# Combining attention heads in six parts, one a slot, with one order of groups and retention outputs a slot later

## The chip, the cores and the metric

The kernel runs on one core of a Trainium2 chip. The metric is the time of one execution in microseconds (us) on the device. The program before took 2319.36 us, the median of three runs (2316.97 to 2319.66).

## The reference

One decoder block on 1024 tokens of width 1024, in fp32. Cut to what matters here:

```python
xn = rmsnorm(x, norm1_g)
qa, ka, va, qr, kr, vr, gr, gate_a, gate_b = split(xn @ w_in)
# mixer A: 12 heads of width 128, three groups of four: (window, dilation) = (128,1), (512,4), (2048,16)
for g in range(3):
    o[g], lse[g] = dilated_group(rmsnorm(qa)[g], rmsnorm(ka)[g], va[g], slopes[g], window[g], dilation[g])
alpha = softmax(stack(lse), axis=0)                    # over the three groups of a head slot
o_a = sum(alpha * stack(o), axis=0)                    # 4 slots of 128
# mixer B: 4 heads, chunks of 128 tokens
s = einsum(q, k) * decay                               # within the chunk: a mask of powers of the decay
out = s @ v + (q @ state) * xi                         # output of a chunk
state = state * g_chunk + (k * zeta).T @ v             # update
o_r = head_groupnorm(out, g, b) * silu(gr)
y = sigmoid(gate_a) * (o_a @ w_proj_a) + sigmoid(gate_b) * (o_r @ w_proj_b)
x = x + y @ w_out
x = x + relu(rmsnorm(x, norm2_g) @ w_up) ** 2 @ w_down
```

## The kernel before

Every large product is split: each fp32 operand is a sum of a high and a low part (`xh`, `xl`; `wh`, `wl`), and three matmuls (high by high, high by low, low by high) replace one. `split` makes the parts: ScalarE copies the high part (L287), VectorE subtracts it (L288). Weights stream from DRAM through three raw buffers and six split buffers (`W`), with 4 units for an attention head.

The stages follow one another: normalisation, attention, the gates, retention, projection a (of attention), projection b (of retention), the output projection, and the MLP.

TensorE's order is the program's. A `Pipe` gives it a form: each `pipe.step` is a slot, one accumulation group (24 matmuls in attention, 12 in projection a), and `pipe.at(lag, fn)` asks for small work that depends on an earlier group, such as transposes, scores and values, to be issued between the terms of the slot `lag` slots after the next. The other engines' instructions are ordered by a list scheduler that has its own estimates, so the place of a line in the program sets their order only loosely. SyncE issues the DMAs in that order, and each of these queues is worked off in order: an instruction that waits holds up what stands behind it.

Attention has 12 heads, in four slots of three groups (`heads`). A head has 8 blocks of 128 tokens. Its queries and keys are normalised (`qk`), turned (`turn_qk`, into `qT`, `kT`), and attended in three steps (scores with `s`, turn with `pr` and `pT`, values into `acc`) at lag 2 for group 0. For groups 1 and 2 the lag is 9, because V goes through DRAM (`v_d`) to get its dilated order (`Vd`). `store` writes `acc` to `acc_d` after the last block. When the three heads of a slot are stored, `load_heads` reads half of the tokens of all three back into `at` (four DMAs into one buffer), and `combine` weighs them by their denominators (`w`; its Exp is on ScalarE), mixes them (`oa`, on VectorE), and asks for their turn (`oaT`) and a store to `oa_d`. This is done in two halves in the last head of the next slot; the last slot's are done in the first head of retention.

Retention works through 4 heads of 8 chunks. For a chunk, `sm` is the masked score (`maskT`, L771), split into `smh` and `sml`; `qh`, `ql`, `kzh`, `kzl`, `vh`, `vl` are the other operands. `output` (9 matmuls and the start of the normalisation of `on`) and `update` (6 matmuls) run one slot after the chunk's values, `turn_o` one slot later still; `on` is then turned, gated and stored to `on_d`.

Projection a has 16 half-steps; each multiplies its product in `ms` by a gate tile `s0` (loaded from `sg_d` into four buffers; the profile calls the tile `s`) and stores it to `pa_d`. Beside it, `load_o` loads the rows of `on_d` (`oraw`, two buffers) and splits them for projection b.

Of the kernel before, what the change touches and what calls it, by code (L numbers as in the profile page):

```python
# [10 lines left out]
F = mybir.dt.float32  # L11
# [226 lines left out]
def hybrid_block(ctx: ExitStack, tc: tile.TileContext, a: dict, out: bass.AP):  # L238
# [62 lines left out]


    W = Weights(nc, rawp, wp, split)
    heads = [(slot, g) for slot in range(SLOTS) for g in ((0, 1, 2) if slot < SLOTS - 1 else (1, 2, 0))]
    for slot, g in heads:
        for u in range(4):
            W.add(a["w_att"][g * SLOTS + slot, u])
# [63 lines left out]
    def as_rows(slot):  # L371

        return [x.rearrange("p (s a) b -> p s (a b)", s=2) for x in slot]
# [28 lines left out]

    def combine(s, i, p2b, at):

        w = p2b.tile([P, 6, 4], F, name="w")
        nm = [at[:, :, g, DH] for g in range(3)]
        dn = [at[:, :, g, DH + 1] for g in range(3)]
        nc.vector.tensor_tensor(w[:, 5], nm[0], nm[1], op=OP.min)
# [11 lines left out]
        oa = p2b.tile([P, 4, DH], F, name="oa")  # L420
        for t in range(4):
            nc.vector.tensor_scalar(oa[:, t], at[:, t, 0, :DH], w[:, 0, t:t + 1], None, op0=OP.mult)
            for g in (1, 2):
                nc.vector.scalar_tensor_tensor(oa[:, t], at[:, t, g, :DH], w[:, g, t:t + 1], oa[:, t],
                                               op0=OP.mult, op1=OP.add)

        def turn():
            pt = tr.tile([P, 4, P], F, name="tr")
            for t in range(4):
                nc.tensor.transpose(pt[:, t, :], oa[:, t, :], ident)  # L430
            ot = p2b.tile([P, 512], F, name="oaT")
            nc.scalar.activation(ot, pt.rearrange("p t q -> p (t q)"), AF.Copy)
            nc.sync.dma_start(oa_d[s, :, 512 * i:512 * i + 512], ot)

        return turn


    attn = ExitStack()
# [3 lines left out]
    with ExitStack() as ph:  # L442
# [69 lines left out]
        for head, (slot, g) in enumerate(heads):  # L512
# [57 lines left out]
            for b in range(NT):  # L570
                if b == 1:
                    nc.vector.tensor_scalar(bias, dist[:, 0 if g < 2 else 1, :], -slope * (DIL[g] if g < 2 else 8),
                                            None, op0=OP.mult)
                if head == 0 and b + 2 < NT:
                    norm1(b + 2)
                if head == 1 and b == 4:
                    first.close()
                    cmb = pool(ph, "cmb", 2)
                if head in (4, 7, 10) and b == 6:
                    at = load_heads(head // 3 - 1, 0, cmb)  # L580
                if head in (5, 8, 11) and b in (0, 3):
# [12 lines left out]
                ss = p3.tile([P, 4], F, name="ssa")  # L594
                junk = p3.tile([P, P], F, name="junk")
                for j in range(2):
                    nc.scalar.activation(junk, pm[:, j * DH:(j + 1) * DH], AF.Square, accum_out=ss[:, j:j + 1])
                rsqrt(ss[:, 2:4], ss[:, 0:2], 1.0 / DH)
                qk = p3.tile([P, 2, DH], F, name="qk", bufs=3)
                nc.scalar.activation(V[:, b, :], pm[:, 2 * DH:3 * DH], AF.Copy)  # L600
                nc.vector.tensor_tensor(qk, pm[:, :2 * DH].rearrange("p (a d) -> p a d", a=2),
                                        ss[:, 2:4, None].to_broadcast([P, 2, DH]), op=OP.mult)

                def turn_qk(g=g, b=b, h=h, qk=qk, qT=qT, kT=kT):
                    pt = tr.tile([P, 4, P], F, name="tr")
# [12 lines left out]
                pipe.at(1, turn_qk)  # L618
            if g > 0:
# [4 lines left out]
                                          v_d[h, 512 * nb:512 * nb + 512, :].rearrange("(p r) e -> p r e", r=4))  # L624
                else:
                    nc.sync.dma_start(Vd, v_d[h].rearrange("(p r) e -> p r e", r=8))


    def gate_out(f, d, cs, src):
# [88 lines left out]
    with ExitStack() as ph:  # L718
# [1 line left out]
        p2 = pool(ret, "p22", 2, "right")  # L720
        p2b = pool(ph, "p22b", 2, "right")

        maskT = cp.tile([P, RH, P], F, name="maskT")
        nc.sync.dma_start(maskT, a["c_mask"])
        rc = const.tile([P, 3, RH], F, name="rc")
        nc.sync.dma_start(rc, a["c_ret"])

        gng = cp.tile([P, 2, NF], F, name="gng")
        nc.sync.dma_start(gng, a["ret_gn"])
        ready = {}  # L730

        def load_chunk(n):
# [22 lines left out]
        for h in range(RH):  # L755
# [4 lines left out]
            for c in range(NT):  # L760
# [5 lines left out]
                def decay(c=c, h=h, it=it, qT=qT, kT=kT):  # L766
# [2 lines left out]
                        nc.tensor.matmul(sp[:, :P], kT[:, f], qT[:, f], start=(f == 0), stop=(f == 1))  # L769
                    sm = p2b.tile([P, P], F, name="sm")  # L770
                    nc.vector.tensor_tensor(sm, sp[:, :P], maskT[:, h, :], op=OP.mult)  # L771
                    it["s"] = p2.tile([P, P], R, name="smh"), p2.tile([P, P], R, name="sml")
                    split(*it["s"], sm)
                    if c > 0:
                        it["q"] = p2.tile([P, 2, P], R, name="qh"), p2.tile([P, 2, P], R, name="ql")
                        split(*it["q"], qT)
                    if c < NT - 1:
                        pt = tr.tile([P, 4, P], F, name="tr")
                        for f in range(2):
                            nc.tensor.transpose(pt[:, f, :], kT[:, f], ident)  # L780
                        kzh = p2b.tile([P, 2, P], R, name="kzh")
                        kzl = p2b.tile([P, 2, P], R, name="kzl")
# [57 lines left out]
                it["v"] = p2.tile([P, DV], R, name="vh"), p2.tile([P, DV], R, name="vl")  # L840
                split(*it["v"], pm)
                pipe.at(0, output, update)
                pipe.at(1, turn_o)
                if h == 0 and c in (0, 2):
                    at = load_heads(SLOTS - 1, c // 2, p2b)
                if h == 0 and c in (1, 4):
                    pipe.at(3, combine(SLOTS - 1, c // 4, p2b, at))
                if h == RH - 1 and c >= 4:
                    load_oa(c - 4)


    before = XS[0, 0], XS[1, 0]
    oS = [x for i in range(2) for x in as_rows(XS[i, 1])]
    with ExitStack() as ph:
# [353 lines left out]
```

## Time and profile before

| | |
|---|---|
| median of the runs | 2319.36 us |
| the profiled execution | 2327.33 us, its span 2325.6 us |
| busy share of the span | TensorE 98%, VectorE 50%, ScalarE 40%, GpSimd 4% |
| mean granted clock of TensorE | 0.995 |
| moved by DMA | 303.19 MB, 130 GB/s |

In the lines below, a group or timeline line names line, engine, operation and tiles (output, arrow, inputs). In square brackets stands how long the engine was idle before it, and what ended that. `SPq` is SyncE issuing DMAs, `PEld` TensorE's weight loads. A line of DMA issues ends with KB each and the median us from issue to landing. A granted clock of 1.00 is full speed.

### The profile page before, as it was taken

To read this page: it belongs to the slowest core of one execution; us is meant where nothing else is said; L and a number is where in the kernel's file an instruction comes from. 1 tells how busy PE (TensorE), PEld (TensorE's weight loads), DVE (VectorE), ACT (ScalarE), POOL (GpSimd) and SP (SyncE) were. 2 spreads that over 40 slices of the span, in tenths; PEclk is the share of its full clock that TensorE was granted. 3 is DMA by queue.
4 is the path that set the end of the run, shared out by engine and by line. 5 is a ranking of instruction groups with operands and counts; after the bars stand their busy time and mean duration, and the time that the engine had idled before them with its cause. 6 is when DMAs were issued, how large, how long until landed. Compare 5 with 4: busy or idle time off the path is not lost. (4 is left out here: it accounts for less than half of the span.)

```text
span 2325.6 us, 29822 instructions
## 1 busy us (share of the span) xinstructions
PE 2281.0 (98%) x11060; PEld 1952.9 (84%) x11060; DVE 1165.8 (50%) x2356; ACT 926.2 (40%) x2078; POOL 104.0 (4%) x148
## 2 busy tenths in 40 slices
PE   8999999999999999989999999999999999999999
PEld 7999998998888888868888878888788888888887
DVE  6344445454644445557676752363855555233532
ACT  6444444445343333335455533122566666211010
POOL 1111111110000000000000000000000000000000
PEclk9999999999999999999999999999999999999999
DMA  4212322332233333363433385554254457733601
GB/s 140 82 55 74 105 63 78 96 105 91 68 112 112 117 113 109 100 187 104 123 113 100 104 273 180 164 171 163 83 173 166 167 169 271 288 127 133 234 28 73
DMA packets 186275, 303.19 MB, mean 130 GB/s; under 512 B 13457, under 2 KB 99601, under 8 KB 182034
## 3 DMA queue, kind: packets, MB, share of 16 engines
q1 hardware_dynamic: 186130, 301.29, 39.9%
q8 instruction: 87, 1.43, 0.3%
q14 instruction: 58, 0.48, 0.1%
HBM read 204.68 MB, written 96.57 MB: 130 GB/s over the span
## 5 line engine op out<-in xcount | busy, mean ns | idle before, releaser
L193 PE MATMUL mm<-wh,xh 128*128 128x384 f32 (+1 forms) x1536 | 605.1, 394 | 5.1 <-ACT wh L287 5.1
L193 PE MATMUL mm<-wh,xl 128*128 128x384 f32 (+1 forms) x1536 | 561.7, 366 | 2.4 <-DVE xl L288 2.1
L288 DVE TENSOR_TENSOR wl<-raw,wh 128x1024 fp32r<-128x1024 f32 (+2 forms) x282 | 306.6, 1092 | 423.1 <-ACT wh L287 420.1
L193 PE MATMUL mm<-wl,xh 128*128 128x384 f32 (+1 forms) x1344 | 486.6, 362 | 2.6 <-DVE wl L288 2.6
L287 ACT ACTIVATE wh<-raw 128x1024 fp32r<-128x1024 f32 (+2 forms) x282 | 267.2, 953 | 535.7 <-PE mm L193 272.1
L193 PEld LDWEIGHTS mm<-wh,xh 128*128 128x128 f32 x1536 | 291.5, 190 | 36.6 <-ACT wh L287 5.7
L193 PEld LDWEIGHTS mm<-wh,xl 128*128 128x128 f32 x1536 | 290.4, 189 | 35.5 <-DVE xl L288 3.4
L193 PE MATMUL mm<-xl,wh 128*128 128x512 f32 x848 | 309.7, 390 | 1.7 <-DVE xl L288 1.7
L193 PE MATMUL mm<-xh,wh 128*128 128x512 f32 x848 | 310.1, 390 | 0.0
L193 PE MATMUL mm<-xh,wl 128*128 128x512 f32 x720 | 280.7, 390 | 0.0
L193 PEld LDWEIGHTS mm<-wl,xh 128*128 128x128 f32 x1344 | 256.3, 191 | 24.8 <-DVE wl L288 3.1
L193 PE MATMUL ms<-xh,wh 128*128 128x512 f32 x604 | 238.6, 395 | 3.9 <-DVE s L888 3.8
L193 PE MATMUL ms<-xh,wl 128*128 128x512 f32 x604 | 235.4, 390 | 0.0
L193 PE MATMUL ms<-xl,wh 128*128 128x512 f32 x604 | 235.3, 390 | 0.0
L193 PEld LDWEIGHTS mm<-xl,wh 128*128 128x128 f32 x848 | 159.5, 188 | 35.2 <-DVE xl L288 2.1
L193 PEld LDWEIGHTS mm<-xh,wh 128*128 128x128 f32 x848 | 159.6, 188 | 33.0
L1109 DVE TENSOR_TENSOR Yd<-Yd,mm 128x512 f32<-128x512 f32 x112 | 76.9, 686 | 172.3 <-PE mm L193 172.0
L193 PEld LDWEIGHTS mm<-xh,wl 128*128 128x128 f32 x720 | 135.4, 188 | 28.1
L193 PEld LDWEIGHTS ms<-xh,wh 128*128 128x128 f32 x604 | 113.5, 188 | 30.1 <-DVE s L888 4.2
L193 PEld LDWEIGHTS ms<-xh,wl 128*128 128x128 f32 x604 | 113.4, 188 | 23.8
L193 PEld LDWEIGHTS ms<-xl,wh 128*128 128x128 f32 x604 | 113.5, 188 | 22.4
L539 ACT ACTIVATE pr<-s,acc 128x128 f32<-128x128 f32 (+1 forms) x96 | 43.1, 449 | 149.2 <-DVE acc L537 136.9
(187 smaller groups left out, 2756.4 us busy)
## 6 DMA issues: line engine op xcount, KB each, us to landing
h_d<-hs SPq DMA_DIRECT2D x64, 512.0 KB, 3.9
raw<-in_w_att SPq DMA_DIRECT2D x48, 384.0 KB, 3.9
raw<-in_w_up SPq DMA_DIRECT2D x32, 512.0 KB, 3.9
raw<-in_w_down SPq DMA_DIRECT2D x32, 512.0 KB, 4.4
xh<-h_d SPq DMA_DIRECT2D x12, 1024.0 KB, 7.1
xl<-h_d SPq DMA_DIRECT2D x12, 1024.0 KB, 8.7
sg_d<-sg SPq DMA_DIRECT2D x32, 256.0 KB, 2.0
raw<-in_w_rqk_q SPq DMA_DIRECT2D x16, 512.0 KB, 3.6
```

Source lines behind the costliest of these rows:

```text
L193: self.nc.tensor.matmul(ps, x, y, start=start, stop=stop, skip_group_check=not first)
L287: nc.scalar.activation(dst_h, src, AF.Copy)
L288: nc.vector.tensor_tensor(dst_l, src, dst_h.bitcast(F), op=OP.subtract)
L539: nc.scalar.activation(st["p"][:, :n], s[:, :n], AF.Exp, bias=acc[:, b, DH:DH + 1], accum_out=acc[:, b, DH + 1:DH + 2])
L1109: nc.vector.tensor_tensor(Y[:, t, ns], Y[:, t, ns], pm, op=OP.add)
```

## The change

- The groups of every slot come in the order 1, 2, 0 (before: 0, 1, 2 in the first three slots).
- `combine` gives back six functions: `weigh`, four times `mix`, and `turn_mixed`. In attention the loads of half 0 stand in the slot's first head (block 6) and those of half 1 in its second; from block 1 of the second and third head one function is called in each slot. For the last slot the same is done in retention, half 0 in its first head and half 1 in its second (load at chunk 1, parts from chunk 3).
- `maskT` and two small constants get a pool of their own and are loaded at the end of attention.
- In retention `output` and `update` run one slot later, and so does `turn_o`; their operands get three buffers in place of two, `sr` four in place of three.
- In projection a, `load_o` is called for one row per half-step. Before, it was called for four rows ahead of the first half-step and for four more once the pipe was empty.

```diff
-    heads = [(slot, g) for slot in range(SLOTS) for g in ((0, 1, 2) if slot < SLOTS - 1 else (1, 2, 0))]
+    heads = [(slot, g) for slot in range(SLOTS) for g in (1, 2, 0)]
...
     def combine(s, i, p2b, at):
-        w = p2b.tile([P, 6, 4], F, name="w")
+        st = {}
+        return [lambda: weigh(p2b, at, st), *(lambda t=t: mix(t, at, st) for t in range(4)),
+                lambda: turn_mixed(s, i, p2b, st)]
...
+    mixing = []
+    def mix_next():
+        if mixing:
+            mixing.pop(0)()
+            if len(mixing) == 1:
+                pipe.at(1, mixing.pop())
...
-                if head in (4, 7, 10) and b == 6:
-                    at = load_heads(head // 3 - 1, 0, cmb)
-                if head in (5, 8, 11) and b in (0, 3):
-                    pipe.at(3, combine(head // 3 - 1, b // 3, cmb, at))
-                    if b == 0:
-                        at = load_heads(head // 3 - 1, 1, cmb)
+                if head >= 3:
+                    i = head % 3
+                    if i < 2 and b == 6:
+                        at = load_heads(head // 3 - 1, i, cmb)
+                    if i > 0 and b == 1:
+                        mixing = combine(head // 3 - 1, i - 1, cmb, at)
+                    mix_next()
...
+    cst = ExitStack()
+    cm = pool(cst, "cm", 1)
+    maskT = cm.tile([P, RH, P], F, name="maskT")
+    nc.sync.dma_start(maskT, a["c_mask"])
...
-            sr = p2.tile([P, 4, P], F, name="sr", bufs=3)
+            sr = p2.tile([P, 4, P], F, name="sr", bufs=4)
...
-                    it["s"] = p2.tile([P, P], R, name="smh"), p2.tile([P, P], R, name="sml")
+                    it["s"] = p2.tile([P, P], R, name="smh", bufs=3), p2.tile([P, P], R, name="sml", bufs=3)
...
-                pipe.at(0, output, update)
-                pipe.at(1, turn_o)
-                if h == 0 and c in (0, 2):
-                    at = load_heads(SLOTS - 1, c // 2, p2b)
-                if h == 0 and c in (1, 4):
-                    pipe.at(3, combine(SLOTS - 1, c // 4, p2b, at))
+                pipe.at(1, output, update)
+                pipe.at(2, turn_o)
+                if h < 2:
+                    if c == 1:
+                        at = load_heads(SLOTS - 1, h, p2b)
+                    if c == 3:
+                        mixing = combine(SLOTS - 1, h, p2b, at)
+                    mix_next()
...
         gates = [loaded(pm2, sg_d[0, d, :, cs], "s0") for d, cs in work[:3]]
-        load_o(oS, 0)
+        waiting = [(place, n) for n, place in enumerate(oS)]
...
-                    load_o(as_rows(ES[0]) + as_rows(ES[1]), 4)
+                    waiting += [(place, 4 + n) for n, place in enumerate(as_rows(ES[0]) + as_rows(ES[1]))]
+                if waiting:
+                    place, n = waiting.pop(0)
+                    load_o([place], n)
```

How the instructions lie is shown at three places. The first is VectorE in attention, where the first slot's halves are combined and the next head's weights are split (`oa` are the mixes, `wl` the splits). Before, the start of the second half:

```order
L408 TENSOR_TENSOR w<-at 128x4
L409 TENSOR_TENSOR w<-w,at 128x4
L411 TENSOR_TENSOR w<-w,at 128x4 x3
L296 TENSOR_SCALAR ssa<-ssa 128x2
L413 TENSOR_TENSOR w<-w,at 128x4
L601 TENSOR_TENSOR qk<-mm,ssa 128x256
L415 TENSOR_TENSOR w<-w,at 128x4
L416 TENSOR_TENSOR w<-w 128x4
L415 TENSOR_TENSOR w<-w,at 128x4
L288 TENSOR_TENSOR wl_2545<-raw_2089,wh_2544 128x768
```

After, the end of the first half, and what follows it to the start of the second:

```order
L432 SCALAR_TENSOR_TENSOR oa<-at,w,oa 128x128
L617 TENSOR_TENSOR qk<-mm,ssa 128x256
L432 SCALAR_TENSOR_TENSOR oa<-at,w,oa 128x128
L288 TENSOR_TENSOR wl_2068<-raw_1612,wh_2067 128x768
L288 TENSOR_TENSOR wl_2080<-raw_1633,wh_2079 128x768
L627 TENSOR_SCALAR kT<-tr,gk 128x4x32
L288 TENSOR_TENSOR wl_2097<-raw_1658,wh_2096 128x768
L296 TENSOR_SCALAR ssa<-ssa 128x2
L617 TENSOR_TENSOR qk<-mm,ssa 128x256
L288 TENSOR_TENSOR wl_2109<-raw_2071,wh_2108 128x768
```

Before, three splits of the head stood within the second half; now they stand behind the whole of the first half and ahead of the second. The mixes of a half are together in both programs.

The second place is SyncE at the same point: `acc_d<-acc` stores a head's output, `at<-acc_d` loads it back. Before:

```order
L566 DMA acc_d<-acc 1024x1x130
L400 DMA at<-acc_d 128x3x130 x4
L560 DMA acc_d<-acc 128x8x130
L400 DMA at<-acc_d 128x3x130 x4
L146 DMA raw_2548<-in_w_att 128x768
L146 DMA raw_2560<-in_w_att 128x768
L146 DMA raw_2577<-in_w_att 128x768
L620 DMA v_d<-V 128x8x128
```

After:

```order
L400 DMA at<-acc_d 128x3x130 x6
L146 DMA raw_2071<-in_w_att 128x768
L146 DMA raw_2083<-in_w_att 128x768
L146 DMA raw_2100<-in_w_att 128x768
L636 DMA v_d<-V 128x8x128
L146 DMA raw_2112<-in_w_att 128x768
L400 DMA at<-acc_d 128x3x130
L639 DMA Vd<-v_d 128x4x128 x2
L400 DMA at<-acc_d 128x3x130
```

The second half's four loads stood together; now two of them follow the first half's four, and the other two stand behind weight loads and the store and reload of V.

The third place is SyncE at the start of projection a (`s` are the gate tiles, which the program calls `s0`). Before:

```order
L864 DMA oraw<-on_d 128x1024
L146 DMA raw_12750<-in_w_pa 128x512
L146 DMA raw_12775<-in_w_pb 128x1024
L864 DMA oraw<-on_d 128x1024 x2
L832 DMA on_d<-onT 128x4x128
L870 DMA s_12793<-sg_d 128x512
L870 DMA s_12795<-sg_d 128x512
```

After:

```order
L146 DMA raw_12731<-in_w_pb 128x1024
L851 DMA on_d<-onT 128x4x128
L887 DMA oraw<-on_d 128x1024 x3
L851 DMA on_d<-onT 128x4x128
L887 DMA oraw<-on_d 128x1024
L146 DMA raw_12874<-in_w_pb 128x1024
L887 DMA oraw<-on_d 128x1024
L893 DMA s_12750<-sg_d 128x512
L893 DMA s_12752<-sg_d 128x512
```

Before, the loads of `oraw` began before the stage; now all five of the first ones stand together, directly ahead of the first gate tiles.

More of the change, by code (lines that the diff above doesn't have):

```diff
@@ L403, in combine, with weigh @@
     def combine(s, i, p2b, at):
-        w = p2b.tile([P, 6, 4], F, name="w")
+        st = {}
+        return [lambda: weigh(p2b, at, st), *(lambda t=t: mix(t, at, st) for t in range(4)),
+                lambda: turn_mixed(s, i, p2b, st)]
+    def weigh(p2b, at, st):
+        w = st["w"] = p2b.tile([P, 6, 4], F, name="w")
+        st["o"] = p2b.tile([P, 4, DH], F, name="oa")
         nm = [at[:, :, g, DH] for g in range(3)]
@@ L419, in combine, with mix, turn_mixed @@
             nc.vector.tensor_tensor(w[:, g], w[:, g], w[:, 4], op=OP.mult)
-        oa = p2b.tile([P, 4, DH], F, name="oa")
-        for t in range(4):
[L422 to L435, printed above, removed]
+    def mix(t, at, st):
+        w, oa = st["w"], st["o"]
+        nc.vector.tensor_scalar(oa[:, t], at[:, t, 0, :DH], w[:, 0, t:t + 1], None, op0=OP.mult)
+        for g in (1, 2):
+            nc.vector.scalar_tensor_tensor(oa[:, t], at[:, t, g, :DH], w[:, g, t:t + 1], oa[:, t],
+                                           op0=OP.mult, op1=OP.add)
+    def turn_mixed(s, i, p2b, st):
+        pt = tr.tile([P, 4, P], F, name="tr")
+        for t in range(4):
+            nc.tensor.transpose(pt[:, t, :], st["o"][:, t, :], ident)
+        ot = p2b.tile([P, 512], F, name="oaT")
+        nc.scalar.activation(ot, pt.rearrange("p t q -> p (t q)"), AF.Copy)
+        nc.sync.dma_start(oa_d[s, :, 512 * i:512 * i + 512], ot)
+    mixing = []
[4 more added lines that the diff above has]
+                pipe.at(1, mixing.pop())
     attn = ExitStack()
@@ L626, in hybrid_block @@
                     nc.sync.dma_start(Vd, v_d[h].rearrange("(p r) e -> p r e", r=8))
+    cst = ExitStack()
+    cm = pool(cst, "cm", 1)
+    maskT = cm.tile([P, RH, P], F, name="maskT")
+    nc.sync.dma_start(maskT, a["c_mask"])
+    rc = cm.tile([P, 3, RH], F, name="rc")
+    nc.sync.dma_start(rc, a["c_ret"])
+    gng = cm.tile([P, 2, NF], F, name="gng")
+    nc.sync.dma_start(gng, a["ret_gn"])
     def gate_out(f, d, cs, src):
@@ L721, in hybrid_block @@
         p2b = pool(ph, "p22b", 2, "right")
[L723 to L729, printed above, removed]
         ready = {}
@@ L771, in decay @@
                     nc.vector.tensor_tensor(sm, sp[:, :P], maskT[:, h, :], op=OP.mult)
-                    it["s"] = p2.tile([P, P], R, name="smh"), p2.tile([P, P], R, name="sml")
+                    it["s"] = p2.tile([P, P], R, name="smh", bufs=3), p2.tile([P, P], R, name="sml", bufs=3)
                     split(*it["s"], sm)
                     if c > 0:
-                        it["q"] = p2.tile([P, 2, P], R, name="qh"), p2.tile([P, 2, P], R, name="ql")
+                        it["q"] = p2.tile([P, 2, P], R, name="qh", bufs=3), p2.tile([P, 2, P], R, name="ql", bufs=3)
                         split(*it["q"], qT)
@@ L780, in decay @@
                             nc.tensor.transpose(pt[:, f, :], kT[:, f], ident)
-                        kzh = p2b.tile([P, 2, P], R, name="kzh")
-                        kzl = p2b.tile([P, 2, P], R, name="kzl")
+                        kzh = p2b.tile([P, 2, P], R, name="kzh", bufs=3)
+                        kzl = p2b.tile([P, 2, P], R, name="kzl", bufs=3)
                         nc.scalar.activation(kzh, pt[:, :2], AF.Copy, scale=rc[:, 2, h:h + 1])
@@ L839, in hybrid_block @@
                     pm = values(us, ts, c == NT - 1)
-                it["v"] = p2.tile([P, DV], R, name="vh"), p2.tile([P, DV], R, name="vl")
+                it["v"] = p2.tile([P, DV], R, name="vh", bufs=3), p2.tile([P, DV], R, name="vl", bufs=3)
                 split(*it["v"], pm)
-                pipe.at(0, output, update)
-                pipe.at(1, turn_o)
-                if h == 0 and c in (0, 2):
-                    at = load_heads(SLOTS - 1, c // 2, p2b)
-                if h == 0 and c in (1, 4):
-                    pipe.at(3, combine(SLOTS - 1, c // 4, p2b, at))
+                pipe.at(1, output, update)
[6 more added lines that the diff above has]
+                    mix_next()
                 if h == RH - 1 and c >= 4:
                     load_oa(c - 4)
+    cst.close()
     before = XS[0, 0], XS[1, 0]
@@ L893, in hybrid_block @@
                     ES = [slot_of(ext) for _ in range(3)] + [slot_of(pool(e1, "ext1", 1, "right"))]
-                    load_o(as_rows(ES[0]) + as_rows(ES[1]), 4)
+                    waiting += [(place, 4 + n) for n, place in enumerate(as_rows(ES[0]) + as_rows(ES[1]))]
+                if waiting:
+                    place, n = waiting.pop(0)
+                    load_o([place], n)
+        assert not waiting
         other = places + as_rows(ES[2]) + as_rows(ES[3])
```

## The prediction

> **What bounds the kernel now.** I read the page first, then TensorE's waits, then the stretches around the longest of them, and last the timelines of SyncE and VectorE there.
>
> ```profile
> span 2325.6 us, 29822 instructions
> PE 2281.0 (98%) x11060; PEld 1952.9 (84%) x11060; DVE 1165.8 (50%) x2356; ACT 926.2 (40%) x2078; POOL 104.0 (4%) x148
> ```
>
> TensorE is busy for 2281.0 of 2325.6 us, and the change takes no matmul away. So it can win at most the 44.6 us in which TensorE idles, and the time in which the matmuls run slowly because it idled just before. The table of TensorE's waits says whose the idle time is (in all, times, longest):
>
> ```profile
> PE ms L193 <- ACT smh L287: 8.5, 1, 8.5
> PE mm L193 <- ACT wh L287: 5.1, 2, 3.4
> PE mm L193 <- DVE xl L288: 3.8, 4, 1.7
> PE ms L193 <- DVE s L888: 3.8, 3, 2.9
> PE mm L193 <- DVE wl L288: 2.6, 2, 1.3
> PE ms L193 <- DVE vl L288: 2.0, 3, 0.9
> PE ms L552 <- DVE pT L547: 1.7, 2, 1.5
> PE ms L545 <- ACT pr L539: 1.5, 2, 1.1
> ```
>
> The change aims at nearly all of these: `wh`, `wl`, `pT`, `pr` are the combines in attention, `smh` the mask, `vl` retention, `s` the gates in projection a, `xl` the first heads. What idle time costs beyond itself shows in stretches chosen around it (length, busy times, then the granted clock, DMA share, GB/s):
>
> ```profile
> 208.51:226.61 18.10, 18.10 (x109) 17.95 (x109) 7.44 (x36) 4.91 (x26) 2.07 (x3) 1.00 0.44 103
> 232.92:236.33 3.41, 3.41 (x13) 3.41 (x12) 2.83 (x12) 1.04 (x3) 0.73 (x1) 0.50 0.82 221
> 358.88:369.98 11.10, 6.37 (x28) 5.70 (x28) 5.70 (x24) 4.05 (x11) 1.42 (x2) 0.85 0.34 96
> 1028.22:1038.46 10.24, 5.83 (x14) 4.58 (x15) 5.00 (x20) 1.26 (x4) 0.56 (x1) 0.50 0.59 182
> 1342.60:1392.20 49.60, 45.13 (x196) 35.84 (x195) 26.90 (x35) 13.16 (x19) 0.55 (x1) 1.00 0.88 281
> ```
>
> The first stretch is four undisturbed groups of 24 matmuls, 4.5 us each. The third is one group beside a combine: 11.1 us. The second and fourth run at half clock. A stretch of 3.41 us at half clock does 1.7 us of work, so it costs 1.7 us. The second follows waits of 1.67 and 1.29 us.
>
> The Trainium skill ("TensorE: Matmul & The Clock Gate", section "HAM oscillation — how this bites in real kernels") gives the rule that TensorE should have no idle gap above about 3.4 us. The trace differs: two gaps of under 1.7 us were enough. Where page and trace part, I go by the trace.
>
> **Combines in attention: today.** SyncE stores the last group's output, loads it back (`at`), and VectorE waits for it:
>
> ```profile
> 204.94 0.52 SPq L566 DMA_DIRECT2D acc_d<-acc  x1
> 209.48 2.56 SPq L400 DMA_DIRECT2D at<-acc_d  x4
> 216.26 0.17 DVE L408 TENSOR_TENSOR w<-at 128x4 f32<-128x4 f32 x1 [5.23 <-DMA at<-acc_d]
> 221.86 1.13 DVE L424 SCALAR_TENSOR_TENSOR oa<-at,w,oa 128x128 f32<-128x128 f32 x4
> 362.82 0.17 DVE L408 TENSOR_TENSOR w<-at 128x4 f32<-128x4 f32 x1 [5.61 <-DMA at<-acc_d]
> 364.57 0.45 PE L193 MATMUL mm<-wh,xh 128*128 128x384 f32 x1 [3.44 <-ACT wh L287]
> 365.29 0.95 DVE L288 TENSOR_TENSOR wl<-raw,wh 128x768 fp32r<-128x768 f32 x1
> acc_d<-acc SPq DMA_DIRECT2D x2, 520.0 KB, 5.4
> at<-acc_d SPq DMA_DIRECT2D x8, 195.0 KB, 3.8
> raw<-in_w_att SPq DMA_DIRECT2D x48, 384.0 KB, 3.9
> ```
>
> VectorE works in order, so what stands behind a late `at` waits too. The first combine of a pair (216.26 to 222.99) stops nobody, since no weight split stands behind it. The second does: ScalarE's Exp in the combine waits, the split `wh` behind it is late, TensorE idles 3.44 us, then for `wl`. The six combines' share of the waits (`wh`, `wl`, `pT`, `pr`) is 5.1 + 2.6 + 1.7 + 1.5 = 10.9, of which I count 10.7, and three stretches at half clock add 3 x 1.7: **15.8 us** that this part could win.
>
> **Combines: after.** In the program text the pieces stand one per group. On VectorE they don't: weigh and the four mixes stand together, the first combine now directly ahead of the next head's weight splits, the second ahead of the first scores of the head. So the first combine gets a deadline that it did not have. Take T0 as the issue of the store.
> - `at` is there at T0 + 5.4 (landing) + 2.6 (four issues) + 4.2 (212.04 to 216.26) = T0 + 12.2. Weigh and mixes with the work between them took 6.7 us; two more pieces of normalisation stand among them now, 0.7. The split `wl` is 0.95. Ready: T0 + 20.5.
> - The store is issued about 1.8 us into the fifth group of a head, so the next head begins at T0 + 16.3 (four groups of 4.5), and the late split feeds its third weight unit, half a group on: T0 + 18.5. Stall: 2.0 us, and half clock after it one time in two: 0.85.
> - The second combine's loads: two wait on SyncE until the first has read its buffer (T0 + 19.6). The last stands behind weight loads that wait for the splits, and behind a store and reload of V. The store of V can go when three splits have freed their buffers, T0 + 23.3, and lands at 28.7 if it takes the 5.4 of the other store; the reload takes 1.2 to issue, and the last `at` lands 3.8 later, near T0 + 33.5. Behind it on VectorE stand the first scores of the head, and behind the combine's Exp on ScalarE their probabilities: ready some 2.7 us later (my estimate: 1.0 for the small operations ahead of Exp, as 362.82 to the split `wl` is 2.5 with more between, the rest for scores and probabilities). TensorE wants them at 16.3 + 2.0 + three groups and 1.7, T0 + 33.5. Stall 2.7, with 0.4 for `pT` behind the mixes, and half clock 1.7: 4.8. Had V landed in 3.9, as a weight load does, the stall would be 1.2.
>
> That is 7.65 per slot, 23.0 for the three, against 15.8: **+7.2 us**. Bounds: if everything lands 2.7 us sooner nothing stalls (-15.8); if each stall is that much longer, +16 more.
>
> **Order of groups.** Group 0 attends within its own head, and no longer does in the first head, where VectorE is short (the `xl` wait, 3.8 in four). The same matmuls return later. **-1.5**, bounds 0 and -2.4.
>
> **Mask.**
>
> ```profile
> 1027.36 0.33 SPq L724 DMA_DIRECT2D maskT<-in_c_mask  x1
> 1031.94 0.29 DVE L771 TENSOR_TENSOR sm<-ms,maskT 128x128 f32<-128x128 f32 x1 [2.30 <-DMA maskT<-in_c_mask]
> 1032.63 0.80 PE L193 MATMUL ms<-vh,smh 128*128 128x512 f32 x1 [8.47 <-ACT smh L287]
> ```
>
> The load is issued as retention starts and TensorE waits 8.47 us for what hangs on it. Then 5.83 us of matmuls run at half clock, 2.9 us lost. Now the load is issued in attention's last head, whole stages early; what stands behind it on SyncE waits for nothing new. **-11.4 us**; at least -8.5, and no more than all of it with the following group, -13.6.
>
> **Retention a slot later.** The three waits for `vl` (2.0 in all) get a whole group of slack; the third buffers keep that from blocking, and no engine gets more work. **-1.5**, bounds 0 and -2.0. The last slot's combine, placed differently among the chunks, waits for no one in TensorE's table: 0.
>
> **Projection a.** The price here is what the move pushes into this stage.
>
> ```profile
> 1343.40 1.46 SPq L864 DMA_DIRECT2D oraw<-on_d  x2
> 1345.56 4.83 SPq L870 DMA_DIRECT2D s<-sg_d  x4
> 1344.43 0.60 ACT L797 ACTIVATE on<-ms 128x512 f32<-128x512 f32 x1 [1.44 <-PE ms L193]
> 1347.20 0.55 DVE L804 TENSOR_SCALAR on<-on,st 128x512 f32<-128x512 f32 x1
> 1351.40 1.06 ACT L287 ACTIVATE xl<-oraw 128x1024 fp32r<-128x1024 f32 x1
> 1342.16 1.21 DVE L288 TENSOR_TENSOR xh<-oraw,xh 128x1024 fp32r<-128x1024 f32 x1
> 1351.62 1.36 DVE L888 TENSOR_TENSOR s<-s,ms 128x512 f32<-128x512 f32 x2 [0.25 <-DMA s<-sg_d]
> 1374.61 0.50 PE L193 MATMUL ms<-xh,wh 128*128 128x512 f32 x1 [2.91 <-DVE s L888]
> 1359.00:1371.00 12.00, 12.00 (x55) 9.94 (x54) 1.00 0.87 292
> s<-sg_d SPq DMA_DIRECT2D x9, 256.0 KB, 6.0
> oraw<-on_d SPq DMA_DIRECT2D x4, 512.0 KB, 5.5
> pa_d<-s SPq DMA_DIRECT2D x7, 256.0 KB, 5.0
> ```
>
> A matmul is 0.22 us (12.00 / 55), a half-step of 12 is 2.6. Today the gate tiles `s` are asked for 3 us into the stage and used at 9; TensorE has banks for three products meanwhile and loses 49.60 - 45.13 = 4.5 us in the whole stage. After: five loads of `oraw` stand ahead of the first four gate loads on SyncE, and the first waits for a matmul of the state update that now runs in the stage's first slot, at t = 6.4 (2.6 + an output of 9 matmuls, 2.0, + an update of 6, 1.3, + a turn). Two land at t = 12.0 and 12.7. The third waits for a split of the first by ScalarE and VectorE (1.06 + 1.21: t = 14.4) and lands near 19.9, the fifth waits for a split of the third. So the gates are issued at t = 21 to 23 and used at t = 27.5 (6.0, less where fewer loads run beside it).
> - The last chunk's normalisation stands behind two of these splits on each engine. ScalarE copies `on` until t = 14.2 + 0.6, VectorE ends its splits near 15.8, and its part took 2.7 (1345.03, the copy's end, to 1347.75): t = 18.5. TensorE wants it at 13.5 (two half-steps and a part, an output, two turns): stall 5.0.
> - TensorE gets to the fourth product at t = 20 and has no bank before t = 27.5: stall 7.5, half clock once, 1.7.
> - Then four buffers turn round in 6.0 + 0.7 + 5.0 = 11.7 us against 4 x 2.6 = 10.4 of matmuls: 3.3 over the rest, as the 2.91 today.
>
> 5.0 + 7.5 + 1.7 + 3.3 = 17.5 against 4.5: **+13 us**. Bounds: -4.5 if the loads flow as the text has them, and +18 with 3 us more on the landings.
>
> **The sum.** 7.2 - 1.5 - 11.4 - 1.5 + 13.0 = +5.8 us. The profiled run took 2327.33 us, 0.3% above the median of the runs, 2319.36; I carry the difference over: **2325.2 us**. About 0.2% (4.6 us) is what a measurement of this kernel can tell from no change, so the forecast lies just beyond it.
>
> **Rivals.**
> 1. Faster, by one mechanism: the `at` loads land within TensorE's slack, from 2.7 us sooner than I put them. Then all attention stalls go: -15.8 in place of +7.2, in all -17, 2302 us. For: four tenths of the chain is landing time, which runs from 3 to 6 us here. Against: VectorE waited for `at` at each of the last combines. 0.17.
> 2. The gates come in time: they are issued before t = 13 or so, and projection a stays at 4.5. Then -7.2, 2312 us. For: the text asks for them first. Against: SyncE's order. 0.14.
> 3. Both: everything goes that the change aims at. -30, 2289 us. 0.07.
> 4. Stalls of 2 to 3 us leave the clock at full speed, so that the combines cost 7.65 less: -1.9, 2317.5 us, no change. Against: 1.67 + 1.29 us were followed by half clock. 0.04. This is what the page of the Trainium skill named above would make of it, with its 3.4 us.
> 5. Worse: landings as slow as the medians in the full stage, and half clock after every stall: +20, 2339 us. 0.10.
>
> My forecast has 0.48. Slower by over 0.2%: most of that and rival 5, 0.55. Within 0.2%: rival 4, the edge of the forecast and of rival 2, 0.13. Faster: rivals 1 to 3, 0.32. The range that leaves out rival 3 and the far end of rival 5 is 2300 to 2342; the forecast's own is 2318 to 2333.
>
> **What would show it.** Right: no wait of TensorE at `smh`; waits for `wl` or `wh` at the head after each first combine and for `pr` after each second; half clock there; in projection a one wait near 5 us for `on` and one of 6 to 9 us for `s`, with the gate loads issued over 18 us into the stage. Wrong: `at` landing before VectorE gets to it, gate loads issued within 13 us, or a new wait at the start of retention where the mask's was.

## The result: slower by 0.66%, and the profile after

The changed kernel takes 2334.03 us (median of 4 runs, 2332.43 to 2337.28), the kernel before 2319.51 us beside it. The ratio is 1.0066, with a 95% interval of 1.0049 to 1.0084: 15 us slower, between 11 and 19. In later runs the kernel before had medians of 2322.1 to 2322.5 us; all differences below are ratios to the runs beside them, times 2322.

The direction was forecast. Most of the amount was not: the waits came much as worked out, but they nearly cancel. What made the kernel slower is a cause that the prediction does not contain. From the page of the changed kernel, and the four of TensorE's waits that the change bears on (in all, times, longest):

```profile
span 2333.7 us, 29807 instructions
PE 2291.3 (98%) x11060; PEld 1953.6 (84%) x11060; DVE 1164.0 (50%) x2356; ACT 923.4 (40%) x2078; POOL 103.6 (4%) x148
PE ms L560 <- ACT pr L554: 11.0, 3, 4.1
PE ms L193 <- DVE s L911: 6.7, 1, 6.7
PE mm L193 <- DVE wl L288: 2.8, 3, 1.2
PE tr L844 <- DVE on L823: 2.7, 3, 1.9
```

TensorE idles 42.4 us of the span (2333.7 - 2291.3), against 44.6 before. It is busy for 10.3 us longer, with the same 11060 matmuls. So the loss is not in the waits, and with a mean granted clock of 0.994 (0.995 before) little of it can be in the clock. It shows in stretches without any idle time: length, busy time and number of matmuls, granted clock, DMA share, GB/s. First the kernel before, then the changed one:

```profile
700.00:800.00 100.00, 100.00 (x443) 1.00 0.35 112
1400.00:1500.00 100.00, 100.00 (x443) 1.00 0.49 164
2100.00:2200.00 100.00, 100.00 (x443) 1.00 0.55 192
```

```profile
700.00:800.00 100.00, 100.00 (x436) 1.00 0.34 113
1400.00:1500.00 100.00, 100.00 (x436) 1.00 0.49 161
2100.00:2200.00 100.00, 100.00 (x443) 1.00 0.46 165
```

In the gates and in the projections TensorE gets through 436 matmuls of 128x512 in 100 us, where it got through 443: 229 ns each in place of 226, at a granted clock of 1.00 in both, with no engine to wait for. In the MLP's second half the rate is the old one. The mean durations of single matmuls in the gates (640 to 990 us) show it unevenly: all six groups were at 389 or 390 ns before; after, four are at 392 to 396 and two stay. Here are the one that grew most and one that stayed, before and after:

```profile
L193 PE MATMUL mm<-xh,wh 128*128 128x512 f32 x292 | 113.6, 389 | 0.0
L193 PE MATMUL mm<-xl,wh 128*128 128x512 f32 x292 | 113.6, 389 | 0.0
```

```profile
L193 PE MATMUL mm<-xh,wh 128*128 128x512 f32 x288 | 113.9, 396 | 0.0
L193 PE MATMUL mm<-xl,wh 128*128 128x512 f32 x288 | 112.0, 389 | 0.0
```

Stage by stage, by the starts of each stage's first matmul in the two profiled runs (2325.6 and 2333.7 us):

| stage | before | after | difference |
|---|---|---|---|
| up to the gates | 540.3 | 541.1 | +0.8 |
| gates | 481.7 | 487.1 | +5.4 |
| retention and projection a | 370.1 | 364.6 | -5.5 |
| projection b to the second normalisation | 230.5 | 234.4 | +3.9 |
| the rest | 703.0 | 706.6 | +3.6 |

The stages that the change touches (the first and third rows) are 4.7 us shorter together; those that it doesn't touch are 12.9 us longer. (This profiled run of the kernel before was 7.8 us above the median of its runs, that of the changed kernel 1.5, so the runs differ by more than the two profiles.)

### The profile page after: what moved, and what is told of

The parts are those of the page before. It is cut to its first block, busy times and chain, and to the rows that moved or that the text cites. A ratio compares the mean times of both kernels' runs of the same rounds, so it can differ in the third digit from the quotient of the medians.

```text
span 2333.7 us, 29807 instructions
## 1 busy us (share of the span) xinstructions
PE 2291.3 (98%) x11060; PEld 1953.6 (84%) x11060; DVE 1164.0 (50%) x2356; ACT 923.4 (40%) x2078; POOL 103.6 (4%) x148
## 4 chain that ended last, share of the span: by engine, by line
PE 90%; DMA 3%; DVE 3%; issue 1%; ACT 1%; SPq 1%; POOL 1%; POOLq 0%; DVEq 0%; ACTq 0%
PE mm L193 63%; PE ms L193 21%; PE ms L547 1%; PE ms L567 1%; DMA at<-acc_d 1%; PE tr L623 1%; PE ms L560 1%; DMA v_d<-V 1%; PE tr L844 1%; PE ms L788 1%; DMA acc_d<-acc 0%; DVE xl L288 0%; ACT xh L287 0%; SPq L400 0%; DVE wl L288 0%
## 5 line engine op out<-in xcount | busy, mean ns | idle before, releaser
L193 PE MATMUL mm<-xh,wh 128*128 128x512 f32 x848 | 314.8, 396 | 0.0
```

Of the source, the lines that this page charges most:

```text
L193: self.nc.tensor.matmul(ps, x, y, start=start, stop=stop, skip_group_check=not first)
```

## Experiments

Two kinds of theory stood against each other. In the first, only waits matter, and the slower matmuls are an accident of one profile. In the second they are real, and set by where the operands lie in memory, or by some state of TensorE that an earlier stage leaves. For placement there was a suspect: the constant `rc`, 48 bytes a partition, had moved out of the pool `const`, which lies below all weights (`wh`, `wl`) and the large operands (`xh`, `xl`) of the left side. All of these start 64 bytes lower in the changed kernel (`wh0` at 29344 in place of 29408). The tiles allocated from the right side, among them a part of `xh`, `xl` in the gates, stay.

### The constant back, and the constant alone

```diff
-    rc = cm.tile([P, 3, RH], F, name="rc")
+    rc = const.tile([P, 3, RH], F, name="rc")
```

That is the edit to the changed kernel; the one to the kernel before is the reverse:

```diff
-        rc = const.tile([P, 3, RH], F, name="rc")
+        rc = cp.tile([P, 3, RH], F, name="rc")
```

> The changed kernel with one constant (rc, 48 bytes a partition) back in the pool of constants, so that every weight and operand tile lies where it did before the change, 64 bytes higher than in the changed kernel. Theory placement (the 3.6 ns by which most 128x512 matmuls of the changed kernel are longer come from where the operands lie): 10 us less than the changed kernel, about 2324 us, and 443 matmuls per 100 us in the gates and the MLP's first half, as before. Theory pacing by state (the longer matmuls are a state of TensorE that some earlier stall sets, wherever the tiles lie): 2334 us, with 436 per 100 us again. Theory stalls (only waits matter, the longer matmuls are an accident of that one profile): 2334 us and 443.

> The kernel before with only that constant moved out of the pool of constants, so that all weight and operand tiles lie 64 bytes lower, as in the changed kernel; same instructions, same order. Theory placement: 10 us more than before, about 2330 us, with 436 matmuls per 100 us in the gates. Theories state and stalls: 2319.5 us, no change beyond 0.2%.

The changed kernel with `rc` back took 2321.48 us, ratio 0.9999 (0.9990 to 1.0008): no slower than before. The kernel before with nothing but `rc` moved took 2335.19 us, ratio 1.0056 (1.0044 to 1.0069): 13 us slower. The same stretch in the profiles of these two, in this order:

```profile
700.00:800.00 100.00, 100.00 (x443) 1.00 0.37 118
```

```profile
700.00:800.00 100.00, 100.00 (x435) 1.00 0.34 111
```

That settles the main question. The loss comes from the constant's move, alone and in the whole change; everything else in the change is worth nothing on balance (-0.2 us, between -2.3 and +1.9).

### What about the addresses

```diff
+    pad = const.tile([P, 16], F, name="pad")
     half = const.tile([P, 2], F, name="half")
```

> The kernel before with all operand tiles 64 bytes higher in place of 64 lower (an unread pad of 64 bytes among the constants). If what counts is the address of these tiles in steps of 128 bytes, 64 up is as 64 down: 13 us more, 436 matmuls per 100 us in the gates. If it is something that depends on the distance of these tiles to others that did not move: 2322 us, as before, or any other value between.

The pad is 64 bytes here, and nothing reads it. 64 bytes up cost as much as 64 bytes down: 2336.32 us, ratio 1.0062 (1.0050 to 1.0074). So it is the address, and not the load of `rc` or its place in the order. The result fits steps of 128 bytes: at 29408 all operands of the gates lie at 96 modulo 128 (the remainder of the address divided by 128, called its residue below), those of the right side too; moved by 64, the left ones lie at 32. So I made all operands one residue modulo 128, retention's too, on the fastest combination of the parts (below). The edit has two pads of 64 bytes each, below the large tiles of the left side.

```diff
+    pad_a = const.tile([P, 16], F, name="pad_a")
     ident = const.tile([P, P], F, name="ident")
+    pad_b = const.tile([P, 16], F, name="pad_b")
...
-                    mx = p3.tile([P, 1], F, name="mx")
+                    mx = p3.tile([P, 16], F, name="mx")[:, :1]
...
```

`ssa`, `w` and `at` are made larger in the same way.

> The same with every operand of a matmul at the same address modulo 128 (96): four small tiles and a pad are made larger, which moves the identity, qk, oa, kzh and kzl by 32 or 64 bytes; all others stay. Theory residue (TensorE streams at 226.7 ns a 128x512 matmul while both operands of all matmuls around have one residue modulo 128, and at 230 ns in stretches where they differ): retention, which mixes residues in all kernels so far, drops from 231 to 227 ns, 5 to 6 us less, and attention may gain too. Rival (retention is slow because of its small matmuls, not of addresses): no change against the kernel beside it.

The expectation took the large tiles to stay, but the pads moved them by 128 bytes. The run went the other way: 2311.15 us (ratio 0.9953, 0.9940 to 0.9965) against 2299.88 for the kernel beside it, with the gates slow. The theory of 128 bytes fell. The move by 128 itself looked like the harm, so I tried a pad of 64 floats on the kernel before, 256 bytes: then every residue modulo 256 is kept.

> The kernel before with all weight and operand tiles of the left side 256 bytes higher (an unread pad). Moves by 64 and by 128 bytes have cost 12 to 14 us. Theory residue, now modulo 256 (TensorE streams at 226.7 ns a 128x512 matmul while all operands around lie at one address modulo 256, and slower where they differ; a move by 256 keeps every residue): 2322 us, as before, 443 matmuls per 100 us in the gates. Rival (any move of these tiles against the tiles that stay costs it): 2335 us, 436.

2322.12 us, ratio 1.0000 (0.9991 to 1.0009), and the old rate. The stretch in the three kernels: 64 up, the one with 128 up, 256 up:

```profile
700.00:800.00 100.00, 100.00 (x435) 1.00 0.33 110
```

```profile
700.00:800.00 100.00, 100.00 (x435) 1.00 0.35 112
```

```profile
700.00:800.00 100.00, 100.00 (x443) 1.00 0.34 109
```

The row +128 is the run on the best parts, the others are the kernel before with that move alone or none:

| left tiles moved by | residue of left and right tiles modulo 256 | matmuls in 700:800 |
|---|---|---|
| 0 | 224, 224 | 443 |
| -64 | 160, 224 | 435 |
| +64 | 32, 224 | 435 |
| +128 | 96, 224 | 435 |
| +256 | 224, 224 | 443 |

In the gates, the projections and the MLP all kernels here fit one rule: a stretch is fast where all its operands lie at one address modulo 256. It explains the MLP's second half, which reads left tiles alone: it is fast in all of them, though these tiles lie at 160, 32 or 96 in the moved kernels. So what counts is that the residues agree, not which one it is. A last run put the rule to use: in the kernel before, retention mixes residues (`ident` and `kzh` at 160, `on`, `vh`, `smh` at 96, `Sh`, `ql` and the weights at 224), and its matmuls are longer than those of the gates. Here all were given 224, while the large tiles stay.

```diff
     half = const.tile([P, 2], F, name="half")
+    rc = const.tile([P, 3, RH], F, name="rc")
     ident = const.tile([P, P], F, name="ident")
...
-                    st = p2.tile([P, 12], F, name="st")
+                    st = p2.tile([P, 32], F, name="st")[:, :12]
...
```

`w` and `at` are larger too.

> The kernel with the early mask and the combine in parts with two buffers, and with the identity and all operands of retention's matmuls at the residue of all others, 224 modulo 256 (the constants in another order, three small tiles made larger; the large tiles of weights and operands stay). Theory residue modulo 256: the gates stay at 226.7 ns and retention drops from 231.5 to 227 ns, 5 to 6 us less than without it, about 2294 us. Rival (retention's matmuls are slow because small ones stand between them): 2300 us, 231 ns as in the other kernels.

Two groups of retention's own matmuls (1060 to 1290 us), first without, then with the alignment:

```profile
L193 PE MATMUL ms<-Sh,ql 128*128 128x512 f32 x40 | 15.8, 395 | 0.0
L193 PE MATMUL ms<-vh,kzh 128*128 128x512 f32 x40 | 15.7, 393 | 0.0
```

```profile
L193 PE MATMUL ms<-Sh,ql 128*128 128x512 f32 x42 | 16.3, 389 | 0.0
L193 PE MATMUL ms<-vh,kzh 128*128 128x512 f32 x42 | 16.3, 389 | 0.0
```

They fall to the 389 ns of the gates. Of these four only `vh` and `kzh` were moved; `Sh` and `ql` lay at 224 in both kernels, and were slower while the matmuls around them mixed residues. The mean from one 128x512 matmul's start to the next falls in retention from 231.5 to 229 ns, about half of the 5 ns expected. The time is 2296.45 us (ratio 0.9891, 0.9876 to 0.9907) against 0.9907 (0.9894 to 0.9921) without it: 3 to 4 us less by the medians, with intervals that overlap, so the gain in time is not shown. The rule predicts where the rate changes, but it is not the whole of retention's pace.

### The parts of the change, each alone

All of these leave the large tiles of weights and operands where they were. Mask alone (`maskT` and `gng` in `cm`, `rc` in `const`, all loaded at the end of attention):

```diff
+    cm = pool(cst, "cm", 1)
+    maskT = cm.tile([P, RH, P], F, name="maskT")
+    nc.sync.dma_start(maskT, a["c_mask"])
+    rc = const.tile([P, 3, RH], F, name="rc")
```

> The kernel before with only the mask and its two companions loaded at the end of attention (tiles of weights and operands where they were). The prediction's term: 11.4 us less (8.5 to 13.6), about 2308 us, no wait at smh and no half clock at the start of retention. Rival (another load is late there next, such as the last combine's or the first queries): 3 to 6 us less.

2312.39 us, ratio 0.9958 (0.9945 to 0.9970): 9.8 us less. At the start of retention TensorE is busy throughout at full clock. A little later it waits once for `on`, for 1.7 us, where it did not before. Its waits for `on` are 2.4 in all, against 0.7 before (length, busy time, clock, then the wait):

```profile
1016.00:1032.00 16.00, 16.00 (x79) 1.00 0.74 218
PE tr L828 <- DVE on L807: 2.4, 2, 1.7
```

The order of groups and the combine in parts in attention, as in the change's diff, with retention's part of the combine run at one go:

```diff
-                    pipe.at(3, combine(SLOTS - 1, c // 4, p2b, at))
+                    parts = combine(SLOTS - 1, c // 4, p2b, at)
+                    for part in parts[:5]:
+                        part()
+                    pipe.at(3, parts[5])
```

> The kernel before with only the order of groups and the combines in parts in attention (the last slot's combine in retention stays where it was). The prediction's term: 7.2 - 1.5 = 5.7 us more, about 2325 us. From the trace of the changed kernel, whose attention ends 0.8 us later than before: 2320 us, with waits for pr of 11 and for wl of 3 us in place of those for wh, wl, pT and pr. If the stalls go in this form: 2304 us.

2324.93 us, ratio 1.0014 (1.0005 to 1.0023): 3.3 us more. The waits for `pr` and `wl`, in the changed kernel 11.0 and 2.8, stand here too:

```profile
PE ms L560 <- ACT pr L554: 12.7, 3, 4.8
PE mm L193 <- DVE wl L288: 3.7, 3, 1.9
```

Then what makes the wait for `pr`: two buffers for `at`, so that the second half's loads need not wait for the first half to be mixed.

```diff
-    def load_heads(s, i, p2b):
-        at = p2b.tile([P, 4, 3, DH + 2], F, name="at", bufs=1)
+    def load_heads(s, i, p2b, n=1):
+        at = p2b.tile([P, 4, 3, DH + 2], F, name="at", bufs=n)
...
-                        at = load_heads(head // 3 - 1, i, cmb)
+                        at = load_heads(head // 3 - 1, i, cmb, 2)
```

> The combine-alone kernel with two buffers for at in attention in place of one, so that the second half's loads follow the first's without waiting for it to be mixed. Theory of the prediction (TensorE's waits for pr, 12.7 us, come from the second half's loads being late behind the first half and the loads of weights and V): these waits and their half clock go, about 14 us less than the combine-alone kernel, 2309 to 2312 us. Rival (the mixes themselves stand in the way of the first scores, however early the loads): no more than 3 us less.

2306.81 us, ratio 0.9936 (0.9924 to 0.9948): 14.9 us less than before and 18 less than with one buffer. All eight loads go out together, and VectorE gets to the second half at 184 us where it waited until 201 in the changed kernel:

```profile
171.17 5.51 SPq L400 DMA_DIRECT2D at<-acc_d  x8
184.00 0.16 DVE L415 TENSOR_TENSOR w<-at 128x4 f32<-128x4 f32 x1
PE mm L193 <- DVE wl L288: 4.0, 3, 1.6
```

No wait for `pr` is left. So the order of groups and the parts together were sound (neither ran alone); a buffer too few turned their gain into a new wait.

The mask with retention's lags and buffers:

```diff
-                pipe.at(0, output, update)
-                pipe.at(1, turn_o)
+                pipe.at(1, output, update)
+                pipe.at(2, turn_o)
```

> The early mask and retention's outputs a slot later, nothing else; operands where they lay before. The mask alone gave -9.7 us. The prediction's terms for the later outputs are -1.5 in retention and +13 in projection a, on top of it: +2, about 2324 us. From the trace of the changed kernel (projection a took 8 to 11 us longer than before, retention's waits for vl are gone): 2319 us, with a wait of 6 us for the first gate product and 2 us for on. Rival (the row-by-row loading of projection a is what makes the gates late, not the later outputs): 2309 us, no such waits.

2320.03 us, ratio 0.9992 (0.9983 to 1.0001). With the mask's 9.8 us taken off, the later outputs cost 8 us (some 4 either way). Their wait is that of the changed kernel, though here rows are loaded as before:

```profile
PE ms L193 <- DVE s L893: 6.3, 2, 5.7
1339.16 0.32 SPq L869 DMA_DIRECT2D oraw<-on_d  x1
1339.53 2.79 SPq L875 DMA_DIRECT2D s<-sg_d  x4
```

The rows of projection a alone:

```diff
-        load_o(oS, 0)
+        waiting = [(place, n) for n, place in enumerate(oS)]
...
+                if waiting:
+                    place, n = waiting.pop(0)
+                    load_o([place], n)
```

> The kernel before with only the loading of rows in projection a spread over the half-steps. If the later outputs are the cause of the late gates: no change, 2322 us within 0.2%, since SyncE still asks for two rows before the stage. If the spreading is the cause: 5 to 8 us more, with a wait of several us for the first gate product.

2321.98 us, ratio 0.9999 (0.9990 to 1.0008): nothing, and no late first gate product:

```profile
PE ms L193 <- DVE s L888: 2.5, 3, 1.9
```

The spreading of rows neither helps nor harms here; the later outputs, with their buffers, push the gates back without it.

The parts add up: -9.8 + 3.3 + 7.9 - 0.2 = +1.2 us, and the changed kernel with its tiles in place gave -0.2 (-2.3 to +1.9).

### The parts that pay, together

The mask's edit, the combine's and the second buffer of `at`, and nothing of retention's lags:

```diff
+    maskT = cm.tile([P, RH, P], F, name="maskT")
...
+    heads = [(slot, g) for slot in range(SLOTS) for g in (1, 2, 0)]
...
+                        at = load_heads(head // 3 - 1, i, cmb, 2)
```

> The early mask with the combine in parts and two buffers for at; retention's outputs and projection a as before. The parts alone gave -9.7 and -15.4 us. If they add: 2297 us. If the early mask's gain came in part from work that the combines left over: 2300 to 2303 us. Operand tiles lie as before the change.

2299.88 us, ratio 0.9907 (0.9894 to 0.9921): 21.6 us less than before. The parts gave 24.7 alone, so they add up nearly. With retention aligned it has the lowest median here, 2296.45 us.

## Why the prediction was right and wrong, step by step

**The sum missed a term.** It gave +5.8 us and the runs gave +15. The terms that it had add up to about +1 on the chip; the +13 of the placement were not in it. The wide range (2300 to 2342) held the result, the forecast's own (2318 to 2333) did not, and the sign was right by luck: with the tiles in place the same edits came out as no change. The step that failed is the list of what the change moves. It was taken from the order of instructions and from buffer counts; of the constants that move with the mask only the load was considered, and TensorE's pace was taken as given ("the change takes no matmul away"), so that the stages which the change does not touch were put at nothing. What the runs showed in its place: moving `rc` out of `const` moves every large tile of the left side by 64 bytes, TensorE gets through 435 matmuls in 100 us in place of 443 in those stages, and this alone costs 13 us.

**Combines: right mechanism, term a little too large (+7.2 forecast, -1.5 for the order of groups, +5.7 for both; +3.3 measured, 1.2 to 5.3).** The first slot of the changed kernel, against the steps:

```profile
166.99 0.38 SPq L575 DMA_DIRECT2D acc_d<-acc  x1
177.79 0.17 DVE L415 TENSOR_TENSOR w<-at 128x4 f32<-128x4 f32 x1 [4.67 <-DMA at<-acc_d]
185.00 1.82 DVE L288 TENSOR_TENSOR wl<-raw,wh 128x768 fp32r<-128x768 f32 x2
186.00 0.44 PE L193 MATMUL mm<-wl,xh 128*128 128x384 f32 x1 [1.00 <-DVE wl L288]
201.07 0.17 DVE L415 TENSOR_TENSOR w<-at 128x4 f32<-128x4 f32 x1 [6.39 <-DMA at<-acc_d]
203.19 0.37 PE L560 MATMUL ms<-ident,pr 128*128 128x128 f32 x1 [4.13 <-ACT pr L554]
203.50:206.90 3.40, 3.40 (x12) 0.52 0.00 0
```

With T0 at 166.99, `at` was there at T0 + 10.8 (12.2 forecast) and the split began at T0 + 18.0 and ended by 19.0 (20.5), so the first stall was 1.0 us, not 2.0. The second `at` was there at T0 + 34.1 (33.5), and the wait for `pr` was 4.1, then 3.9 and 3.0 in the other slots (2.7), each followed by half clock. Two errors of opposite sign, small beside the landing times that they rest on. The loads' queue, named as the cause, is confirmed by the second buffer. The term for the order of groups does not show: TensorE's wait for `xl`, which it was to shorten, was 3.8 us in four before, and 3.5 in four in the changed kernel, 3.7 with the combines alone.

**The clock.** The first slot's wait of 4.13 us was followed by a stretch at 0.52 (last line). In the fastest parts together a single wait of 2.03 us was enough:

```profile
314.45 0.44 PE L193 MATMUL mm<-wl,xh 128*128 128x384 f32 x1 [2.03 <-DVE wl L288]
315.60:318.80 3.20, 3.20 (x13) 0.53 0.90 266
```

So the rival that let waits under 3.4 us go free (the Trainium skill, "TensorE: Matmul & The Clock Gate", section "HAM oscillation — how this bites in real kernels") is not what happens here; the measurement decides. But the length of a wait does not settle it either: the one of 2.91 us at 1374.61 in the kernel before was not followed by half clock (the prediction's row 1342.60:1392.20 has a clock of 1.00). What decides between them was not tried.

**Mask: right (-11.4 forecast, -9.8 measured, -7.0 to -12.8).** The wait at `smh` and the half clock are gone. What the forecast left out is the new wait for `on`, 1.7 us; that is about the difference, which lies within the noise.

**Later outputs: right mechanism, too large in the trace (+13.0 - 1.5 forecast; +8 measured, some 4 either way).**

```profile
1334.87 6.62 SPq L887 DMA_DIRECT2D oraw<-on_d  x3
1348.01 2.63 SPq L893 DMA_DIRECT2D s<-sg_d  x4
1345.99 0.66 PE L844 MATMUL tr<-ident,on 128*128 128x128 f32 x4 [1.93 <-DVE on L823]
1354.40 0.79 PE L193 MATMUL ms<-xh,wh 128*128 128x512 f32 x1 [6.73 <-DVE s L911]
1354.40:1360.00 5.60, 5.60 (x13) 0.50 0.87 293
```

The stage's first matmul starts at 1328.0. From the first `oraw` to the gates' issue it is 13.1 us (14.6 to 16.6 forecast), the wait for the first product is 6.7 (7.5), followed by half clock (5.6 us at 0.50 cost 2.8; 1.7 forecast). The wait for `on` was 1.9, not 5.0: the first rows landed sooner than the 5.5 us taken, and TensorE got there at 1344.1, some 16 us into the stage (13.5 forecast). The later turnaround of the four buffers, put at 3.3, cost nothing: no second wait for `s` is in the table.

**Rivals.** Attention without stalls (rival 1) needed the loads 2.7 us sooner; in the change as it stands the first came 1.4 us sooner and the second 0.6 later, so the rival fell. With a second buffer VectorE got to the second half 17 us sooner, and then 14.9 of its 15.8 us came. The gates in time (rival 2) is refuted by the changed kernel's own trace, where they were issued 20.0 us into the stage, and by the later outputs' run. The worst case (rival 5, 2339 us) lies nearest to the measured time, but by waits that did not come. No rival had a cost outside the stages that the change touches.

## What to carry to other kernels

When an edit moves an allocation, look at what else moves with it: 48 bytes taken from the lowest pool cost 13 us, more than the largest gain of the change (the mask's 9.8). Compare TensorE's matmuls per 100 us in stretches without idle time, in stages that the change does not touch, before explaining a difference by waits. And an operation spread over slots gains nothing while its loads share one buffer: the queue in front of the buffer decides when it starts, not its place in the text.

## What the runs showed of the hardware

- The rate at which TensorE streams 128x512 matmuls depended on the addresses of its operands: 443 in 100 us when all tiles in use lay at one address modulo 256, 435 or 436 when left and right tiles differed by 64 or 128, at the same granted clock of 1.00. A move of the left side by 256 cost nothing (ratio 1.0000). What in the hardware does this wasn't tried, nor moves that are no multiple of 64, nor whether other sizes of matmul or other types pay it.
- In the changed kernel the slower rate sets in some 85 us into the gates, where the first tiles from the right side are read: from the start of one matmul to the next it is 226.7 ns between 580 and 620 us and about 230 from 630 on. From there on groups that read left tiles alone are slow too, until the MLP's second half, which reads left tiles only (443 in 2100:2200).
- One wait of 2.0 us was followed by some 3.4 us at half clock, as were waits of 3.0, 3.9 and 4.1; one of 2.9 us was not.
